# Key projection of a two-layer RWKV7/NSA kernel: one 512-column matmul per piece of high weight, halves summed by VectorE

## The chip, the cores and the metric

The kernel runs on one core of a Trainium2 chip. A core has a matmul engine (TensorE, PE in the profile; its weight loads are listed apart as PEld), three engines that compute on tiles (VectorE, DVE; ScalarE, ACT; GpSimd, POOL) and SyncE (SP), which here only issues transfers. The engines run side by side, each through its own instructions in order, and wait for one another through semaphores. Matmul results go to PSUM: eight banks, each of 512 float32 columns on 128 partitions. Everything else on the chip lies in SBUF.

The metric is the device time of one execution in microseconds. The time before is the median of three runs.

## The reference

256 tokens of width 2048 go through an RWKV7 layer, then an NSA attention layer that shares one set of keys and values, then a norm. The change lies in the RWKV7 layer, in the projection that makes the keys:

```
xx = token_shift(u) - u
mixed = u[None] + xx[None] * mu[:, None, None, :]
rkvz = jnp.einsum('nbtd,nde->nbte', mixed[:4], w_rkvz)
r, k, v, z = rkvz[0], rkvz[1], rkvz[2], rkvz[3]
...
kk = heads(k * k_k).astype(jnp.float32)
kk = kk / jnp.maximum(jnp.sqrt(jnp.sum(kk * kk, axis=-1, keepdims=True)), 1e-12)
k = k * (1.0 + (a - 1.0) * k_a)
...
o = wkv7_scan(rh, heads(decay), kh, vh, -kk, kk * ah.astype(jnp.float32))
```

Everything is float32. k has 2048 columns, that is 16 blocks of 128, two heads of 64 in each.

## The kernel before

**Products.** TensorE multiplies float32 in a rounded form (fp32r). To keep precision, each operand is split in two: a rounded, "high" part and the "low" rest. A product is the sum of three: high weight by high input, high weight by low input, low weight by high input. A weight piece arrives by DMA in a tile wraw; ScalarE writes its rounded copy whi (line 211) and VectorE the rest, wlo (line 190). Five pairs of whi and wlo exist, so the splitting runs some three pieces ahead of TensorE. For the inputs, function split_into makes the same two parts, and puts them side by side in one tile mx of 2 x 256 columns; the dictionary joint keeps that tile under the name of the projection and the 128-row piece k.

**Order of the work.** First all of v; then z block 0 (512 columns), the sixteen key blocks, z blocks 1 to 3, and then the scan, into which the projection of r is dealt. The list ZK holds that middle part. For one key block, cols_step runs four times, once for each 4 pieces of 128 rows; for each piece it issues three matmuls of 256 columns (tokens) into a 128 x 256 result with the weights stationary. cols_step also has a second form: given an output of 512 columns, it multiplies whi by the whole joint tile (512 columns: high and low input side by side), and wlo by the high input into the first 256 columns. The z blocks of the second layer use that form already, and VectorE adds the two halves behind it (line 1733).

**Key stage.** When a key block is done, stage_k takes it up: it copies it out of PSUM (ksb), squares it (sqk), sums squares by head on TensorE (rn, line 699), takes the power -0.5 (line 707 VectorE, 708 GpSimd), spreads it (rnx, line 714 ScalarE and 717 TensorE), and makes the tile sp of scaled keys, decays and inverse decays (lines 720 to 737, on VectorE, ScalarE and GpSimd), of which TensorE makes products ab (line 744). Stage j begins when block j is done and stage j - 2 has made its ab. The stages of several blocks overlap with the next blocks' matmuls.

**Triangular inverse.** When stages 0 to 7 are through, stage_t(0) reads their products back from DRAM (invA) and inverts triangular 32 x 32 matrices with small VectorE instructions (inverse_ops, line 774); its result goes out to DRAM (tnd, yvd) and comes back for the scan (Yb, line 883, used by TensorE at line 998). stage_t(1) does the same for blocks 8 to 15.

**What sets the order of instructions.** The generator code runs under a small planner, Sched, that interleaves stages, mixing of inputs (lines 426, 427, 433) and matmuls by planned costs. On top of it the framework's scheduler simulates the engines in time and lays out the final order of each engine. So a changed instruction can move others on all engines.

**PSUM.** In this part, acc tiles turn through banks 2, 0 and 1. Two key blocks share one bank: block j in the first 256 columns if j is even, in the last 256 if it is odd. A z block takes two banks. When a z block is done, ScalarE and VectorE evacuate it (close_z, line 647).

## Time and profile before

| | us |
|---|---|
| Median of three runs | 1145.06 |
| Lowest, highest | 1141.73, 1147.56 |
| Profiled execution, its own time | 1145.28 |
| Its span in the profile | 1143.5 |
| First key block's first matmul starts | 144.4 |
| Last key block's last matmul of the first kind (line 595) starts | 276.6 |
| The scan's first matmul of line 998 starts | 365.3 |

The page of a profile gives the busy time of each engine and its share of the span. A matmul row of a timeline gives its start and its length; the lengths of neighbouring matmuls overlap, since they are pipelined. "PEclk" is the clock that TensorE was granted, as a share of full speed. In square brackets stands the time that an engine sat idle before an instruction, and what ended it. A row with "x16: 361/366/375" gives the count, and the least, median and longest duration in ns.

### The profile page before, as it was taken

The numbers are of one execution on the slowest core, as the hardware profiler recorded it, in microseconds if no ns is written. First come the engines' busy times: TensorE is split into PE (matmuls) and PEld (weight loads), VectorE is DVE, ScalarE is ACT, GpSimd is POOL, SyncE is SP. The second block draws the span as 40 slices with busy tenths as digits, with TensorE's granted clock in tenths as the row PEclk, the third lists the DMA queues.
The fourth block names the chain that finished last, engine by engine and source line by source line (L and its number), as shares of the span: only waits on it lengthen the run. The fifth ranks groups of instructions, "written<-read, shape, count | busy, mean of one in ns | idle before, by whom it ended". The sixth has DMA issues, their size and how long they took to land.

```text
span 1143.5 us, 24949 instructions
## 1 busy us (share of the span) xinstructions
PE 1113.6 (97%) x9136; PEld 962.9 (84%) x9136; DVE 864.4 (76%) x1807; ACT 715.3 (63%) x1680; POOL 346.9 (30%) x443
## 2 busy tenths in 40 slices
PE   8999999999999999999999999999999999999997
PEld 7788899988688988888778888787889988888787
DVE  7999976779978986556666877675576888988564
ACT  5667777767655465556556766664666666666553
POOL 1400045554434365444110010100334344452212
PEclk9999999999999999999999999999999999999999
DMA  6568978885899978665457758585756453748462
GB/s 227 169 189 233 250 205 245 227 219 173 265 282 276 240 196 236 170 172 137 139 183 224 234 166 284 164 291 167 187 152 162 117 149 105 198 108 283 166 194 102
DMA packets 238522, 225.37 MB, mean 197 GB/s; under 512 B 57541, under 2 KB 184821, under 8 KB 238400
## 3 DMA queue, kind: packets, MB, share of 16 engines
q1 hardware_dynamic: 233120, 217.17, 65.0%
q0 software_dynamic: 5280, 6.61, 2.1%
q8 instruction: 72, 1.18, 0.5%
q14 instruction: 50, 0.41, 0.1%
HBM read 200.48 MB, written 23.10 MB: 196 GB/s over the span
## 4 chain that ended last, share of the span: by engine, by line
PE 62%; DVE 5%; DMA 2%; issue 2%; ACT 1%; POOL 1%; POOLq 0%; ACTq 0%; DVEq 0%
PE bank L576 9%; PE bank L577 9%; PE bank L579 9%; PE bank L601 5%; PE bank L1285 3%; PE bank L602 3%; PE bank L241 2%; DMA Yb<-yvd 2%; PE bank L1286 2%; PE bank L1287 2%; DVE wlo L190 2%; PE pair L1304 2%; PE pair L1306 1%; PE pair L1305 1%; PE pair L241 1%
## 5 line engine op out<-in xcount | busy, mean ns | idle before, releaser
L190 DVE TENSOR_TENSOR wlo<-wraw,whi 128x512 fp32r<-128x512 f32 (+2 forms) x616 | 448.9, 744 | 150.4 <-ACT whi L211 147.8
L211 ACT ACTIVATE whi<-wraw 128x512 fp32r<-128x512 f32 (+2 forms) x664 | 402.7, 620 | 232.9 <-PE bank L579 91.7
L577 PE MATMUL bank<-wlo,mx 128*128 128x512 f32 (+3 forms) x576 | 217.8, 380 | 3.5 <-DVE wlo L190 2.6
L579 PE MATMUL bank<-whi,mx 128*128 128x512 f32 (+3 forms) x576 | 215.0, 376 | 0.0
L576 PE MATMUL bank<-whi,mx 128*128 128x512 f32 (+3 forms) x576 | 186.5, 377 | 1.3 <-ACT whi L211 0.5
L577 PEld LDWEIGHTS bank<-wlo,mx 128*128 128x128 f32 x576 | 108.7, 189 | 22.8 <-DVE wlo L190 5.4
L576 PEld LDWEIGHTS bank<-whi,mx 128*128 128x128 f32 x576 | 107.9, 189 | 19.1 <-ACT mx L1869 1.2
L579 PEld LDWEIGHTS bank<-whi,mx 128*128 128x128 f32 x576 | 108.7, 189 | 16.2 <-POOL mx L1870 0.4
L190 POOL TENSOR_TENSOR wlo<-wraw,whi 128x512 fp32r<-128x512 f32 (+2 forms) x48 | 63.1, 1316 | 110.6 <-ACT whi L211 88.7
L601 PE MATMUL bank<-mx,whi 128*128 128x512 f32 x240 | 86.8, 398 | 0.0
L595 PE MATMUL bank<-mx,whi 128*128 128x256 f32 (+1 forms) x288 | 85.0, 295 | 0.3 <-ACT mx L426 0.3
L596 PE MATMUL bank<-mx,whi 128*128 128x256 f32 (+1 forms) x288 | 82.3, 286 | 0.0
L597 PE MATMUL bank<-mx,wlo 128*128 128x256 f32 (+1 forms) x288 | 81.7, 286 | 0.0
L1285 PE MATMUL bank<-mx,whi 128*128 128x256 f32 x256 | 81.6, 319 | 0.0
L577 PE MATMUL bank<-wlo,kvh 128*128 128x512 f32 x192 | 76.9, 401 | 0.0
L579 PE MATMUL bank<-whi,kvl 128*128 128x512 f32 x192 | 76.1, 396 | 0.0
L1286 PE MATMUL bank<-mx,whi 128*128 128x256 f32 x256 | 72.9, 285 | 0.0
L1287 PE MATMUL bank<-mx,wlo 128*128 128x256 f32 x256 | 72.8, 284 | 0.0
L602 PE MATMUL bank<-mx,wlo 128*128 128x256 f32 x256 | 70.6, 285 | 0.2 <-DVE wlo L190 0.2
L576 PE MATMUL bank<-whi,kvh 128*128 128x512 f32 x192 | 67.4, 396 | 0.0
L426 ACT ACTIVATE mx<-mtmp 128x256 fp32r<-128x256 f32 x96 | 38.7, 413 | 31.1 <-DVE mtmp L433 30.8
L595 PEld LDWEIGHTS bank<-mx,whi 128*128 128x128 f32 (+1 forms) x288 | 54.0, 187 | 2.2 <-ACT mx L426 0.7
(344 smaller groups left out, 2393.8 us busy)
## 6 DMA issues: line engine op xcount, KB each, us to landing
wraw<-in_a_w_rkvz_dram SPq DMA_DIRECT2D x128, 512.0 KB, 5.4
wraw<-in_kv_w_dram SPq DMA_DIRECT2D x48, 512.0 KB, 4.4
wraw<-in_b_w_in_dram SPq DMA_DIRECT2D x40, 512.0 KB, 4.2
wraw<-in_a_w_o_dram SPq DMA_DIRECT2D x32, 512.0 KB, 4.6
wraw<-in_b_w_o_dram SPq DMA_DIRECT2D x32, 512.0 KB, 3.9
spd<-sp SPq DMA_DIRECT2D x16, 642.0 KB, 5.1
wraw<-in_b_w_in_dram SPq DMA_DIRECT2D x24, 384.0 KB, 3.4
spl<-spd SPq DMA_DIRECT2D x14, 642.0 KB, 7.2
```

Of the source, the lines that this page charges most:

```text
L190: eng.tensor_tensor(lv, src, hv.bitcast(F32), op=OP.subtract)
L211: self.nc.scalar.activation(hv, src, AF.Copy)
L576: PE.matmul(o, mh[:, ts], wh[:, 0, :], start=k == ends[0], stop=False)
L577: PE.matmul(o, mh[:, ts], wl[:, 0, :], start=False, stop=False)
L579: PE.matmul(o, ml[:, ts], wh[:, 0, :], start=False, stop=k == ends[1])
L595: PE.matmul(o, wh[:, s, :], mh, start=k == 0 and first, stop=False, **kw)
L596: PE.matmul(o, wh[:, s, :], ml, start=False, stop=False, **kw)
L601: PE.matmul(o, wh[:, s, :], joint[nm, k], start=k == 0, stop=False, **kw)
L602: PE.matmul(o[:, :T], wl[:, s, :], mh, start=False, stop=False, **kw)
L1285: PE.matmul(o, wh[:, s, :], mh, start=k == 0, stop=False)
L1286: PE.matmul(o, wh[:, s, :], ml, start=False, stop=False)
L1287: PE.matmul(o, wl[:, s, :], mh, start=False, stop=k == NK - 1)
```

## The change

The key blocks use the second form of cols_step. Each key block takes a whole bank: whi times the joint tile fills 512 columns, wlo times the high input adds to the first 256. VectorE's reduce adds the two halves into ksb in SBUF, and ScalarE squares ksb, where before ScalarE copied and squared the block from PSUM. Sixteen banks are turned through now in the key part, not eight, over the same three banks.

```diff
         pk = kps.pop(j)
         ksb = tmp("ksb")
         sqk = tmp("t1")
-        S.activation(ksb, pk, AF.Copy)
-        S.activation(sqk, pk, AF.Square, scale=KK[:, j:j + 1])
+        V.tensor_reduce(ksb, pk.rearrange("p (a t) -> p t a", a=2), axis=AX.X, op=OP.add)
+        S.activation(sqk, ksb, AF.Square, scale=KK[:, j:j + 1])
         rn = accp("rn")
...
-    kacc = []
-
     def phase_k(j):
         if j % 2 == 0:
             load_pair(j // 2)
-            kacc[:] = [accp("acc")]
-        o = kacc[0][:, (j % 2) * 256:(j % 2) * 256 + 256]
+        o = accp("acc")
         for q in range(4):
             yield from cols_step(o, "k", q)
```

The form of cols_step that the key blocks take now, and which was there before for the z blocks of the second layer:

```
end = k == NK - 1
if not end:
    PE.matmul(o, wh[:, s, :], joint[nm, k], start=k == 0, stop=False, **kw)
PE.matmul(o[:, :T], wl[:, s, :], mh, start=False, stop=False, **kw)
if end:
    PE.matmul(o, wh[:, s, :], joint[nm, k], start=False, stop=True, **kw)
```

Three lines fewer stand in the file from phase_k on, so line 774 of before is line 771 of after, and so forth.

The order of TensorE at the end of the first key block, before (bank_1777 is the block's bank, mx_1675 and mx_1693 the last two input pieces):

```order
L595 MATMUL bank_1777<-mx_1675,whi 128x256
L596 MATMUL bank_1777<-mx_1675,whi 128x256
L597 MATMUL bank_1777<-mx_1675,wlo 128x256
L595 MATMUL bank_1777<-mx_1693,whi 128x256
L596 MATMUL bank_1777<-mx_1693,whi 128x256
L597 MATMUL bank_1777<-mx_1693,wlo 128x256
L595 MATMUL bank_1777<-mx_1393,whi 128x256
```

And now, at the same place:

```order
L601 MATMUL bank_1777<-mx_1675,whi 128x512
L602 MATMUL bank_1777<-mx_1675,wlo 128x256
L602 MATMUL bank_1777<-mx_1693,wlo 128x256
L604 MATMUL bank_1777<-mx_1693,whi 128x512
L689 MATMUL bank_2050<-hw,w2s 128x256
L690 MATMUL bank_2050<-ha,w2s 128x256
L601 MATMUL bank_1830<-mx_1393,whi 128x512
```

Two matmuls stand where three stood, the last piece closes with the wide one, and the next block goes to another bank (1830) where before it went on in 1777.

The order of VectorE around the first key block's evacuation, before (the two zth rows evacuate z block 0; f, sst and cum belong to the key stage):

```order
L647 TENSOR_TENSOR zth<-bank_1545,zth 128x512
L190 TENSOR_TENSOR wlo<-wraw,whi 128x512 x4
L726 TENSOR_TENSOR f<-ksb,f 128x256
L707 TENSOR_SCALAR sst<-bank_1862 128x4
L711 SCALAR_TENSOR_TENSOR cum<-cst,thw 128x256
```

And now:

```order
L647 TENSOR_TENSOR zth<-bank_1545,zth 128x512
L190 TENSOR_TENSOR wlo<-wraw,whi 128x512 x3
L695 TENSOR_REDUCE ksb<-bank_1777 128x256
L190 TENSOR_TENSOR wlo<-wraw,whi 128x512
L726 TENSOR_TENSOR f<-ksb,f 128x256
L711 SCALAR_TENSOR_TENSOR cum<-cst,thw 128x256
```

The reduce of block 0 stands among the low weights, and the stage's small instructions change places behind it.

The order of VectorE at the end of z block 1, the first z block behind the keys, before (inv names are the triangular inverse, mx and mtmp the mixing of r, zth the evacuation of the z block):

```order
L774 TENSOR_TENSOR invX<-invT,invM 128x512
L190 TENSOR_TENSOR wlo<-wraw,whi 128x512
L433 SCALAR_TENSOR_TENSOR mtmp<-xx,prm,xn 128x256
L647 TENSOR_TENSOR zth<-bank_3811,zth 128x512
L647 TENSOR_TENSOR zth<-bank_3812,zth 128x512
L427 TENSOR_TENSOR mx_4323<-mtmp,mx_4323 128x256
L427 TENSOR_TENSOR mx_4362<-mtmp,mx_4362 128x256
L774 TENSOR_REDUCE invT<-invX 128x8x8
L427 TENSOR_TENSOR mx_4413<-mtmp,mx_4413 128x256
```

And now:

```order
L427 TENSOR_TENSOR mx_4165<-mtmp,mx_4165 128x256
L190 TENSOR_TENSOR wlo<-wraw,whi 128x512
L647 TENSOR_TENSOR zth<-bank_3563,zth 128x512
L771 TENSOR_TENSOR invX<-invA,invM_2757 128x512
L647 TENSOR_TENSOR zth<-bank_3564,zth 128x512
L771 TENSOR_REDUCE invM<-invX 128x8x8
L190 TENSOR_TENSOR wlo<-wraw,whi 128x512
L771 TENSOR_TENSOR invX<-invA,invM_2757 128x512
```

The mixing of r is through at that place, where before three pieces were left; the inverse has come less far: it reads invA here (the first of the last level's two products) where before it read invT (the second).

## The prediction

> **What bounds the kernel now.** First the page: its first two lines and the chain that ended last, to see which engine sets the end.
> ```profile
> span 1143.5 us, 24949 instructions
> PE 1113.6 (97%) x9136; PEld 962.9 (84%) x9136; DVE 864.4 (76%) x1807; ACT 715.3 (63%) x1680; POOL 346.9 (30%) x443
> PE 62%; DVE 5%; DMA 2%; issue 2%; ACT 1%; POOL 1%; POOLq 0%; ACTq 0%; DVEq 0%
> ```
> TensorE (PE) is busy for 1113.6 of 1143.5 us, so time is mostly saved by giving it less to do. That is an average, and the change touches only the sixteen key blocks and what stands behind them. So next the table by stretches, cut where the key blocks begin, where the triangular inverse's first VectorE instruction runs, where the z block behind the keys ends, where VectorE (DVE) gets air again, and where the last z block ends.
> ```profile
> core 0: us, PE busy (x) PEld busy (x) DVE busy (x) ACT busy (x) POOL busy (x), PEclk, DMA share, GB/s
> 144.20:235.60 91.40, 90.91 (x789) 86.11 (x788) 62.47 (x102) 68.49 (x163) 46.88 (x57) 1.00 0.83 227
> 235.60:311.10 75.50, 69.79 (x501) 59.40 (x500) 74.77 (x168) 53.23 (x127) 35.22 (x42) 1.00 0.72 211
> 311.10:320.00 8.90, 8.64 (x31) 6.62 (x31) 8.85 (x15) 4.31 (x8) 5.67 (x11) 0.81 1.08 305
> 320.00:353.70 33.70, 33.70 (x150) 27.91 (x149) 25.66 (x61) 19.70 (x34) 7.03 (x11) 1.00 0.93 268
> ```
> Two regimes. Up to 235.6 us TensorE runs without a gap (90.91 of 91.40) and VectorE has 28.93 us free: the bound is TensorE. From 235.6 to 311.1 VectorE is full (74.77 of 75.50), and TensorE stands for 5.71 us: the bound is VectorE. From 320 us TensorE is the bound again. The ends of the second stretch, and what it costs, in the timeline:
> ```profile
> 235.64 0.19 DVE L774 COPY invT<-invA 128x16 f32<-128x16 f32 x1 [3.33 <-DMA invA<-abd]
> 311.13 1.27 DVE L647 TENSOR_TENSOR zth<-bank,zth 128x512 f32<-128x512 f32 x2
> 309.66 0.50 PE L577 MATMUL bank<-wlo,mx 128*128 128x512 f32 x1 [0.76 <-DVE wlo L190]
> 311.86 0.63 PE L576 MATMUL bank<-whi,mx 128*128 128x512 f32 x1 [0.26 <-DVE zth L647]
> 312.29 0.63 PE L577 MATMUL bank<-wlo,mx 128*128 128x512 f32 x1
> ```
> TensorE waits for a low weight (wlo) and for the evacuation zth, and then its matmuls start 0.43 us apart (311.86, 312.29): the granted clock of 311.1 to 320 is 0.81. So lateness is paid twice there. Last the waits of TensorE from 235 to 320 us, longest first:
> ```profile
> PE bank L744 <- POOL sp L736: 2.7, 2, 2.1
> PE bank L577 <- DVE wlo L190: 1.5, 4, 0.8
> PE bank L717 <- ACT rnx L714: 1.3, 1, 1.3
> PE bank L576 <- DVE zth L647: 0.3, 1, 0.3
> ```
> Only 1.8 us (1.5 + 0.3) name VectorE itself. The other 4.0 are the key stage's own chain (key block, norm, rnx, nk, sp, L744), which passes VectorE's full queue three times; the change puts its reduce at the head of that chain.
>
> **What TensorE saves.** A step is one 128-row piece of one block: three matmuls of 256 columns now, one of 512 and one of 256 afterwards. Both forms stand in this trace, the new one in the z blocks of the second layer (L601, L602). The rows' first number is the start, and matmuls overlap, so the price is the distance of the starts.
> ```profile
> 276.49 0.28 PE L597 MATMUL bank<-mx,wlo 128*128 128x256 f32 x1
> 276.61 0.28 PE L595 MATMUL bank<-mx,whi 128*128 128x256 f32 x1
> 276.73 0.28 PE L596 MATMUL bank<-mx,whi 128*128 128x256 f32 x1
> 276.85 0.28 PE L597 MATMUL bank<-mx,wlo 128*128 128x256 f32 x1
> ...
> 1041.09 0.40 PE L601 MATMUL bank<-mx,whi 128*128 128x512 f32 x1
> 1041.32 0.28 PE L602 MATMUL bank<-mx,wlo 128*128 128x256 f32 x1
> 1041.44 0.40 PE L601 MATMUL bank<-mx,whi 128*128 128x512 f32 x1
> 1041.68 0.28 PE L602 MATMUL bank<-mx,wlo 128*128 128x256 f32 x1
> 1041.79 0.39 PE L601 MATMUL bank<-mx,whi 128*128 128x512 f32 x1
> ```
> Old step: 276.85 - 276.49 = 0.36 us. New step: (1041.79 - 1041.09) / 2 = 0.35 us. The columns streamed are the same 768; what goes is one start. So 0.01 us for each of 16 x 16 = 256 steps: **2.6 us**. The starts are printed to 0.01 us, so the difference may be 0.005 to 0.015: 1.3 to 3.8 us. At most 11 of the 16 blocks (1.8 us) lie before 235.6 us, where TensorE is the bound and the saving counts at once.
>
> [...]
>
> **What ScalarE loses.** The copy of the block out of PSUM goes, and the square reads the SBUF copy.
> ```profile
> L695 ACT ACTIVATE ksb<-bank x16: 361/366/375, 150.8 to 279.5; 128x256 f32<-128x256 f32 x16
> L696 ACT ACTIVATE t<-bank,prm x16: 462/467/478, 151.0 to 279.8; 128x256 f32<-128x256 f32 x16
> L732 ACT ACTIVATE sp<-f,prm x16: 492/510/527, 152.3 to 288.1; 128x256 f32<-128x256 f32 x16
> ```
> 16 x 0.366 = 5.9 us less on an engine that is busy for 68.49 of 91.40 and 53.23 of 75.50 us: worth nothing by itself. The square may grow a little: L732, of the same size with a scale column and both sides in SBUF, takes 0.510 where the square takes 0.467, 0.7 us for sixteen, hidden too.
>
> **What VectorE gains.** Sixteen reduces of 512 to 256 columns out of PSUM. The same instruction evacuates the z blocks of the second layer.
> ```profile
> L1733 DVE TENSOR_REDUCE zT<-bank x16: 673/681/692, 833.0 to 1044.1; 128x256 f32<-128x512 f32 x16
> ...
> 1036.24 0.68 DVE L1733 TENSOR_REDUCE zT<-bank 128x256 f32<-128x512 f32 x1
> 1036.84 0.18 DVE L1793 RECIPROCAL rc<-sm 128x6 f32<-128x6 f32 x1
> ```
> One lasts 0.681 us and the next instruction starts after 0.60 us, so 0.60 us of VectorE's time each, 9.6 us in all. In the new order eleven reduces stand ahead of the inverse's first instruction: 11 x 0.60 = 6.6 us, hidden by the 28.93 us free there (if that cover were gone, the weights' low halves would be 6.6 us late). Each reduce stands in VectorE's queue behind the low weights of the next block (the four of block 1 ahead of block 0's reduce), so while it waits for its own block's last matmul it holds back nothing that TensorE needs in the block after. The other **five, 3.0 us**, fall into the full stretch.
>
> But the order that the scheduler lays out has other work moved in that stretch, too. Between the inverse's first instruction and the first zth I count in the two orders: inverse 66 then 59, low weights 37 then 35, mixing of r 26 then 29, small work of the key stage 39 then 35, reduces 0 then 5. The seven inverse pieces that now stand behind zth are those of 128x512:
> ```profile
> 309.53 0.68 DVE L774 TENSOR_TENSOR invX<-invT,invM 128x512 f32<-128x512 f32 x1
> 310.13 0.68 DVE L190 TENSOR_TENSOR wlo<-wraw,whi 128x512 fp32r<-128x512 f32 x1
> 310.73 0.47 DVE L433 SCALAR_TENSOR_TENSOR mtmp<-xx,prm,xn 128x256 f32<-128x256 f32 x1
> ```
> These rows give 0.60 us (309.53 to 310.13, 310.13 to 310.73) for an inverse piece and for a low weight, and 0.40 (to zth at 311.13) for a mixing piece and, as an upper bound, for a small one. The reduces, the inverse and the mixing give +3.0 - 7 x 0.60 + 3 x 0.40 = **0.0 us**. The two low weights and four small pieces (2 x 0.60 + 4 x 0.40 = 2.8 us) merely moved ahead of the inverse's start, so they come off no total. Bounds: all five reduces unpaid, +3.0; two more low weights' progress won, -2.8. I take 0: VectorE neither loses nor wins there, and what remains is TensorE's earlier arrival.
>
> What is late next is the inverse. Its last piece stands behind low weight 187 instead of 182. TensorE uses six matmuls for one low weight, 6 x 33.70 / 150 = 1.35 us by the table's last row, so 5 x 1.35 = 6.7 us later. Its readers:
> ```profile
> 323.96 1.22 DVE L774 TENSOR_REDUCE invT<-invX 128x64 f32<-128x1024 f32 x1
> L883 SPq DMA_DIRECT2D Yb<-yvd x8: 303/441/642, 338.0 to 343.1; - x8
> L998 PE MATMUL pair<-Yb,a x256: 192/219/240, 365.3 to 537.0; 64*64 64x32 f32 x128
> ```
> The load of Yb goes out 14 us after the last piece (323.96 to 338.0), and TensorE uses it at 365.3. A delay of 6.7 us is inside that margin. SyncE's queue, where weight loads stand behind the Yb load, would be held by it only once the delay passes those 14 us less the stores between. I cost it at nothing.
>
> **Sum.** 2.6 saved on TensorE, of which I take 2.0 as kept (the 1.8 us before 235.6 us and a part of the rest), nothing on ScalarE, nothing net on VectorE: **-2.0 us**. The profiled execution took 1145.28 us (1143.5 of span and 1.8 around it), 0.2 above the median of three, 1145.06. Forecast: 1145.28 - 2.0 = 1143.3 us.
>
> **Rivals.**
> *VectorE eats the gain.* If the full stretch keeps all the inverse's pieces in front of what TensorE waits for in effect, the five reduces push zth 3.0 us out and only the 1.8 us won before remain: 1145.28 + 3.0 - 1.8 = 1146.5 us. For it: the 74.77 of 75.50. Against it: the seven pieces moved behind zth.
>
> *The full stretch relaxes.* If the moved inverse pieces take VectorE off the bound there, some 0.6 of the 5.71 us of standing go (my guess between a third, the 1.8 us that name VectorE, and all), and the lost clock behind zth too, (1 - 0.81) x 8.90 = 1.7 us: 1145.28 - 2.6 - 0.6 x 5.71 - 1.7 = 1137.6 us. For it: those pieces are exactly the work that nobody needs yet. Against it: the mixing of r, as little needed, stays in front.
>
> *Slower: VectorE stands at the reduces.* VectorE's queue is in order. In the full stretch low weights, the inverse and the key stage's own products stand behind a reduce, which must wait for its block's last matmul. The plan was made with planned times; if TensorE reaches that matmul 1.4 us (about one low weight's worth) after VectorE reaches the reduce, five such waits cost 7 us, with 3.0 for the reduces and one more stretch of lost clock, 1.7, less 2.6 saved: 1145.28 + 9.1 = 1154.4 us. It decides from the point where VectorE catches up with TensorE; in the full stretch it has been behind, so this needs the plan to err the other way.
>
> *A 512-column matmul as cheap as one of 256.* If streaming overlapped so far that a wide matmul costs one start, each step would take 0.24 us: 256 x 0.12 = 31 us less, 1114.6 us. The rows speak against it: 1041.09 to 1041.32 is 0.23 for the wide one. [...]
>
> **How the numbers follow.** Forecast 0.50; VectorE eats the gain 0.28; the stretch relaxes 0.12; slower 0.09; the cheap wide matmul 0.01. About 0.5%, 5.7 us, is what a measurement of this kernel can tell from no change. The forecast and the first rival lie inside it; of the second rival three quarters lie beyond it, with the last rival 0.10 for faster; the slower one, whole, and a little of the first give 0.10; 0.80 stay within. The forecast's own range is the bounds of its terms: the saving (-3.8 to -1.3) and -2.8 to +3.0 for the full stretch, 1138.7 to 1147.0. The first rival, with nothing won before 235.6 us and the square's 0.7 added, reaches 1149; so 1139.0 to 1149.0, leaving out the slower rival and the far part of the two fast ones.
>
> **What would show it.** Right, if the new L601 to L601 distance in the key blocks is 0.35 us, the eleven key blocks before the inverse's start take 1 to 2 us less, TensorE's idle time from there to zth is again near 5.7 us, and the reduces last 0.68 us with no wait ahead of them on VectorE in the full stretch. Wrong, if waits of TensorE for L190 or zth grow by more than 3 us, if a reduce shows idle time released by TensorE in the full stretch, or if the scan's first L998 waits for Yb.

## The result, and the profile after

The changed kernel takes 1156.17 us (median of five; 1150.82 to 1158.62) where the kernel before takes 1145.06. The ratio is 1.0098, with a 95% interval of 1.0073 to 1.0124: 11 us slower. The forecast was 1143.3, the range 1139.0 to 1149.0; the time lies outside it. The profiled execution took 1152.86 us, 1151.1 of them span.

First the page's lines, as before:

```profile
span 1151.1 us, 24448 instructions
PE 1116.0 (97%) x8880; PEld 951.8 (83%) x8880; DVE 871.3 (76%) x1823; ACT 709.3 (62%) x1664; POOL 347.1 (30%) x443
PE 58%; DVE 6%; issue 4%; DMA 3%; ACT 2%; POOL 2%; SPq 0%; POOLq 0%; ACTq 0%; DVEq 0%
```

There are fewer matmuls (8880 for 9136), yet TensorE is busy for longer. The table by stretches, with the prediction's cuts and one more at the end, says where:

```profile
core 0: us, PE busy (x) PEld busy (x) DVE busy (x) ACT busy (x) POOL busy (x), PEclk, DMA share, GB/s
144.20:235.60 91.40, 89.57 (x606) 75.57 (x604) 68.22 (x114) 62.42 (x145) 45.01 (x56) 1.00 0.80 220
235.60:311.10 75.50, 69.06 (x402) 55.28 (x401) 70.03 (x165) 52.40 (x126) 34.79 (x37) 0.95 0.70 196
311.10:320.00 8.90, 8.90 (x39) 6.69 (x39) 5.26 (x10) 2.50 (x5) 6.92 (x15) 0.68 0.90 273
320.00:353.70 33.70, 33.70 (x150) 27.89 (x150) 26.74 (x45) 19.92 (x33) 8.11 (x14) 1.00 0.98 272
353.70:380.00 26.30, 21.10 (x170) 19.51 (x171) 20.59 (x58) 11.13 (x21) 10.12 (x17) 0.87 0.98 274
```

The last row of the kernel before, by the same view:

```profile
353.70:380.00 26.30, 25.72 (x375) 24.30 (x374) 24.12 (x57) 13.34 (x27) 14.24 (x25) 1.00 1.07 276
```

Two things are new. TensorE no longer runs without a gap up to 235.6 us (1.83 us free where there were 0.49). And the granted clock (third number from the end) falls to 0.95, 0.68 and 0.87 where it was 1.00, 0.81 and 1.00. TensorE's waits from 235 to 320 us, and from 320 to 380:

```profile
PE bank L744 <- POOL sp L736: 3.5, 3, 2.3
PE bank L717 <- ACT rnx L714: 2.1, 2, 1.4
PE bank L699 <- ACT t L696: 1.1, 1, 1.1
PE bank L577 <- DVE wlo L190: 0.3, 1, 0.3
...
PE bank L1282 <- DVE vt L647: 4.6, 1, 4.6
PE pair L1021 <- ACT bkt L1024: 0.6, 1, 0.6
```

From 320 to 380 us the kernel before has the last of these alone:

```profile
PE pair L1024 <- ACT bkt L1027: 0.6, 1, 0.6
```

The waits for low weights and zth, which the prediction watched, shrank from 1.8 to 0.3 us. The key stage's own waits grew from 4.0 to 6.7, and one of 4.6 us is new, at the first matmul of r's projection. It is the largest single loss, and the prediction had not thought of it:

```profile
361.73 0.68 DVE L647 TENSOR_TENSOR vt<-bank,vt 128x512 f32<-128x512 f32 x1
...
362.47 0.58 PE L1282 MATMUL bank<-mx,whi 128*128 128x256 f32 x1 [4.62 <-DVE vt L647]
362.85 0.42 PE L1283 MATMUL bank<-mx,whi 128*128 128x256 f32 x1
363.06 0.42 PE L1284 MATMUL bank<-mx,wlo 128*128 128x256 f32 x1
```

vt is the evacuation of the last z block (z3). TensorE wants z3's bank for r, and VectorE empties it late. Behind the wait the matmuls start 0.21 us apart instead of 0.12. The windows around the three stretches of half clock, TensorE alone (length, busy, count, granted clock):

```profile
251.99:255.40 3.41, 1.76 (x20) 1.00 0.66 189
255.40:258.82 3.42, 2.95 (x12) 0.50 0.91 213
258.82:262.23 3.41, 3.41 (x12) 0.50 0.78 202
262.23:265.64 3.41, 3.41 (x20) 1.00 0.47 154
306.60:310.02 3.42, 1.21 (x5) 0.99 0.45 156
310.02:313.43 3.41, 3.20 (x20) 0.50 0.50 176
313.43:316.84 3.41, 3.41 (x9) 0.50 0.93 179
357.81:361.22 3.41, 0.04 (x1) 0.99 1.16 291
361.22:364.63 3.41, 2.16 (x10) 0.50 1.16 290
364.63:368.05 3.42, 3.42 (x18) 0.51 1.09 365
```

Cut in steps of 3.41 us from the right point, each of the three windows in which TensorE stands long (busy for 1.76, 1.21 and 0.04 us) is followed by two whole windows at half clock. At the granted 0.50 each of those costs up to half of 3.41, an estimated 1.7 us; six of them make 10.2 us, where the kernel before has one between 140 and 400 us. (Part of one passes while TensorE stands anyway, as at 361.22, so the 10.2 and the waits may not be added up.)

How the lateness builds up can be read from the starts of a few instructions in the two traces (us):

| | before | changed | later by |
|---|---|---|---|
| Key block 11, first matmul | 232.31 | 230.47 | -1.8 |
| Key block 15, first matmul | 269.16 | 271.15 | 2.0 |
| VectorE's first zth of z block 1 | 311.13 | 312.98 | 1.9 |
| r's first matmul, less its wait for vt | 353.71 | 357.85 | 4.1 |
| r's first matmul | 353.71 | 362.47 | 8.8 |
| The first matmul that reads Yb | 365.31 | 376.61 | 11.3 |

Up to block 11 the changed kernel is ahead by what the prediction counted on; all of the loss comes behind that.

### The profile page after: what moved, and what is told of

Read it like the earlier page. It is cut to its first block, busy times and chain, and to the rows that moved or that the text cites. A ratio compares the mean times of both kernels' runs of the same rounds, so it can differ in the third digit from the quotient of the medians.

```text
span 1151.1 us, 24448 instructions
## 1 busy us (share of the span) xinstructions
PE 1116.0 (97%) x8880; PEld 951.8 (83%) x8880; DVE 871.3 (76%) x1823; ACT 709.3 (62%) x1664; POOL 347.1 (30%) x443
## 4 chain that ended last, share of the span: by engine, by line
PE 58%; DVE 6%; issue 4%; DMA 3%; ACT 2%; POOL 2%; SPq 0%; POOLq 0%; ACTq 0%; DVEq 0%
PE bank L577 8%; PE bank L579 8%; PE bank L576 8%; PE bank L601 5%; PE bank L1282 3%; DVE wlo L190 3%; PE bank L602 3%; PE bank L241 2%; PE bank L1283 2%; PE bank L1284 2%; DMA Yb<-yvd 2%; PE pair L1301 2%; PE pair L1303 1%; PE pair L1302 1%; PE pair L241 1%
## 5 line engine op out<-in xcount | busy, mean ns | idle before, releaser
L577 PE MATMUL bank<-wlo,mx 128*128 128x512 f32 (+3 forms) x576 | 218.6, 381 | 3.1 <-DVE wlo L190 2.0
L601 PE MATMUL bank<-mx,whi 128*128 128x512 f32 x480 | 179.1, 408 | 0.0
L602 PE MATMUL bank<-mx,wlo 128*128 128x256 f32 x512 | 141.8, 287 | 0.2 <-DVE wlo L190 0.2
L601 PEld LDWEIGHTS bank<-mx,whi 128*128 128x128 f32 x480 | 91.5, 191 | 18.0
L602 PEld LDWEIGHTS bank<-mx,wlo 128*128 128x128 f32 x512 | 97.9, 191 | 4.3 <-DVE wlo L190 0.7
L1284 PE MATMUL bank<-mx,wlo 128*128 128x256 f32 x256 | 73.1, 285 | 0.0
L1282 PEld LDWEIGHTS bank<-mx,whi 128*128 128x128 f32 x256 | 49.5, 193 | 8.8 <-DVE vt L647 5.0
L1283 PEld LDWEIGHTS bank<-mx,whi 128*128 128x128 f32 x256 | 50.1, 196 | 0.0
```

What stands on the lines that cost most here:

```text
L577: PE.matmul(o, mh[:, ts], wl[:, 0, :], start=False, stop=False)
L601: PE.matmul(o, wh[:, s, :], joint[nm, k], start=k == 0, stop=False, **kw)
L602: PE.matmul(o[:, :T], wl[:, s, :], mh, start=False, stop=False, **kw)
L1282: PE.matmul(o, wh[:, s, :], mh, start=k == 0, stop=False)
L1283: PE.matmul(o, wh[:, s, :], ml, start=False, stop=False)
L1284: PE.matmul(o, wl[:, s, :], mh, start=False, stop=k == NK - 1)
```

## The experiments

All ratios are against runs of the kernel before on the same chip. Since one profiled execution differs from another by some microseconds outside the changed part, the last column gives a local measure from the traces: from VectorE's first zth (the evacuation of z block 0) to the first matmul of the scan that reads Yb. The kernel before has 218.6 us there (146.7 to 365.3), the changed one 229.9, so the loss arises in this part.

| label | what differs | ratio [95% interval] | local, us |
|---|---|---|---|
| (the change) | | 1.0098 [1.0073, 1.0124] | 229.9 |
| e1_rot | change, z blocks in the banks of before | 1.0061 [1.0040, 1.0082] | 224.8 |
| e2_badrot | before, z blocks in the banks of the change | 1.0021 [1.0000, 1.0042] | 219.7 |
| e3_dvecopy | before, VectorE copies the blocks | 1.0053 [1.0030, 1.0076] | 220.3 |
| e4_wide_act | e1, ScalarE evacuates one half | 1.0011 [0.9992, 1.0031] | 218.2 |
| e6_load | e4 and an unread reduce on VectorE | 1.0042 [1.0026, 1.0057] | 221.6 |
| e5_split | e1, ScalarE and VectorE share the sum | 1.0043 [1.0025, 1.0061] | 221.8 |
| e7_narrow_bank | before, a bank for each block | 0.9994 [0.9976, 1.0011] | 216.9 |
| e16_copy_bank | e7, VectorE copies the blocks | 1.0030 [1.0014, 1.0047] | 219.6 |
| e14_sum_early | e4, VectorE sums blocks 0 to 10 | 1.0028 [1.0009, 1.0047] | 219.1 |
| e15_sum_late | e4, VectorE sums blocks 11 to 15 | 1.0060 [1.0037, 1.0083] | 222.3 |
| e8_klag3 | e1, three stages in flight | 1.0058 [1.0033, 1.0082] | 223.6 |
| e9_warm | e4 and idle matmuls | 1.0106 [1.0089, 1.0124] | 225.8 |
| e13_warm_sum | e1 and idle matmuls | 1.0118 [1.0096, 1.0140] | 226.9 |
| e18_sq_dve | e1, VectorE squares too | 1.0138 [1.0107, 1.0169] | 225.8 |
| e19_sq_pool | e1, GpSimd squares | 1.0089 [1.0056, 1.0123] | 224.0 |
| e11_pool | e1, 8 low weights on GpSimd | 1.0055 [1.0038, 1.0071] | 220.6 |
| e12_pool_narrow | e7, 8 low weights on GpSimd | 1.0116 [1.0097, 1.0136] | 227.6 |
| e20_rmix_pool | before, r's low parts on GpSimd | 1.0103 [1.0076, 1.0129] | 226.2 |

**The turn of the banks.** Sixteen turns over three banks end one bank from where eight turns end. So z3 lies in banks 0 and 1, and r's projection begins in just those; before, it lay in 1 and 2. e1 sets the turn back behind the keys, e2 shifts it in the kernel before (with 2 for 1):

```diff
     for nm, i in ZK:
+        if (nm, i) == ("z", 1):
+            turn["acc"] += 1
```

> The changed kernel, but the turn of the three banks is advanced by one ahead of z block 1, so that the z blocks and the scan get the same banks as in the kernel before. Theory A (bank turn): z block 3 lay in banks 0 and 1 in the changed kernel, which the scan's projection of r needs at once, so TensorE stood 4.6 us for vt and then ran some 4 us at half clock. Then the wait for vt is gone, the first r matmul comes 0.2 us behind the last z matmul, and the time is 4 to 7 us under the changed kernel's 1156.2: 1149 to 1152. Rival B (all of the loss comes from the key stage, and the scan takes up the wait anyway, since its Yb loads have less to wait for then): under 1.5 us less, 1155 to 1156.

> The kernel before, with the turn of the banks advanced by two ahead of z block 1, so that z block 3 lies in banks 0 and 1 as in the changed kernel. Nothing else is edited. Theory A: TensorE waits 4 to 5 us for vt ahead of the scan, and the time is 4 to 7 us over the kernel before: 1149 to 1152. Rival B: within 1.5 us of 1145.

e1 is 0.37% faster than the change, 4.2 us (5.1 by the local measure), as theory A forecast, and its wait for vt is gone (one of 2.0 us for a low weight stands behind it instead). In e2 the wait appears:

```profile
PE bank L1287 <- DVE vt L647: 3.0, 1, 3.0
```

It costs only 2.4 us there (0 to 4.8 by the interval), between the two forecasts: VectorE reaches vt at 355.10 us, not 361.73, and no half clock follows. So the bank turn makes the wait, and by these two traces the lateness of VectorE decides its price.

**Who evacuates.** In place of ScalarE's copy and square from PSUM, e3 (two blocks a bank) and e16 (a bank for each) have VectorE's copy with narrow matmuls; e4 has ScalarE with wide ones (first half only); e7 is the narrow kernel with a bank for each block and e1's turn.

```diff
 e3, e16
-        S.activation(ksb, pk, AF.Copy)
-        S.activation(sqk, pk, AF.Square, scale=KK[:, j:j + 1])
+        V.tensor_copy(ksb, pk)
+        S.activation(sqk, ksb, AF.Square, scale=KK[:, j:j + 1])
 e4
-        V.tensor_reduce(ksb, pk.rearrange("p (a t) -> p t a", a=2), axis=AX.X, op=OP.add)
-        S.activation(sqk, ksb, AF.Square, scale=KK[:, j:j + 1])
+        S.activation(ksb, pk[:, :256], AF.Copy)
+        S.activation(sqk, pk[:, :256], AF.Square, scale=KK[:, j:j + 1])
 e7, e16
-        o = kacc[0][:, (j % 2) * 256:(j % 2) * 256 + 256]
+        o = accp("acc")[:, :256]
```

> The kernel before (narrow matmuls, two blocks a bank), with one part of the change: VectorE copies the key block out of PSUM, 256 columns, and ScalarE squares the copy. Theory C (the evacuation at the head of the key stage's chain now stands in VectorE's queue): waits of TensorE in the key blocks for t, rnx and sp (lines 699, 717, 744) grow from 4.5 to 6 us or more, some with half clock behind; time 2 to 4 us over before, 1147 to 1149. Rival D (only the length of the reduce counts, and a copy of 256 columns at about 0.34 us each is hidden): within 1 us of 1145.

> The wide matmul and one bank a block, with the bank turn of e1_rot, but ScalarE evacuates as before, and the first 256 columns alone; the product of high weight and low input in the second half is left out of ksb. This is the change without VectorE's part. If the wide matmul saves its 0.01 us a step and the banks are right, TensorE's 2.6 us come through: 1142 to 1143.5. If instead the order that the scheduler makes of a shorter key block is itself worse (waits of TensorE in the key blocks over 6 us), 1146 or more.

> The kernel before with its three narrow matmuls and ScalarE's copy and square, but with one bank for each key block instead of one for two, and the banks turned back behind the keys: the wide matmul is all that the wide kernel with ScalarE's copy (+1.3 us) has beyond it. If the wide matmul's 2.6 us do not come through since TensorE only waits more for the key stage: 0 to +2 us over the kernel before, 1144.4 to 1146.4. If they do come through, and the bank of its own for each block costs what was won: +3 to +4.5 us, 1147.4 to 1149, with more waits of TensorE from 144 to 311 us than before (6.3 us).

> Narrow matmuls, a bank for each block, the banks turned back, and VectorE's copy of the block (0.42 us) in place of ScalarE's, the square from the copy. Beside the same kernel with ScalarE's copy (-0.6 us) it gives the price of the evacuation by VectorE without wide matmuls a second time, and beside the changed kernel with its banks turned back (+7.0 us) what the wide matmul is worth where VectorE evacuates. If the evacuation costs 5 to 6 us whatever the matmuls' form, and the wide matmul again wins nothing: +4.5 to +6 us over the kernel before. If the wide matmul's 2.6 us come through where VectorE evacuates: +7.5 to +9.5.

VectorE in place of ScalarE costs 0.50% with wide matmuls (e1 less e4), 0.53% (e3) and 0.36% (e16 less e7) with narrow ones: 4 to 6 us, three times. The wide matmul itself wins nothing in either pair: e4 less e7 is +0.17%, e1 less e16 +0.31% (in the second pair the reduce is also longer than the copy, 0.68 to 0.42 us). And a bank of its own for each block costs nothing (e7). Of the forecasts, e3's were both too low (+6.1 us came); e4 lies between its two, and e7 (-0.7) and e16 (+3.4) lie a little below the nearer of theirs.

Why the wide matmul's gain does not come through, e4 shows beside the kernel before (the rows of 200 to 235 and 235 to 260 us, e4's first, then the kernel before's):

```profile
200.00:235.00 35.00, 33.51 (x237) 28.25 (x234) 22.92 (x40) 24.84 (x64) 18.01 (x24) 1.00 0.79 216
235.00:260.00 25.00, 21.89 (x135) 18.62 (x136) 20.33 (x59) 17.86 (x47) 11.48 (x15) 0.88 0.89 226
```
```profile
200.00:235.00 35.00, 35.00 (x307) 32.96 (x307) 23.80 (x39) 27.60 (x68) 19.43 (x25) 1.00 0.84 228
235.00:260.00 25.00, 22.71 (x201) 20.93 (x200) 23.96 (x66) 17.18 (x43) 14.49 (x17) 1.00 0.71 201
```

The gain is there at first. Block 11 begins 84.8 to 86.1 us after the first key matmul in twelve of the thirteen kernels with wide matmuls (87.5 in e13, which has idle matmuls added), and 87.6 to 87.9 us in the seven with narrow ones. It is lost behind that. In e4 TensorE begins block 13 102.7 us after the first key matmul, the kernel before 107.2: e4 is 4.5 us ahead. Then it waits for sp (2.0 us at 252.2) and rnx (1.0 at 255.0), runs at half clock from 254 to 261 us, and needs 14.3 us for that block instead of 9.0. The work in between is the key stage's, which lags: from a block's square to ScalarE's copy of its products ab it took 17.5 to 27 us in e4 for the blocks 0 to 12, and 12.7 to 18.3 before. The wide form's order puts the stage's steps later; why the scheduler does so was not tried.

**How much is VectorE's load, how much the chain.** e6 adds the reduce to e4, into a tile that nobody reads. e5 shortens VectorE's part. e8 lets three stages overlap (KLAG = 3).

```diff
 e6
+        V.tensor_reduce(kdm, pk.rearrange("p (a t) -> p t a", a=2), axis=AX.X, op=OP.add)
 e5
-        V.tensor_reduce(ksb, pk.rearrange("p (a t) -> p t a", a=2), axis=AX.X, op=OP.add)
+        S.activation(ksb, pk[:, 256:], AF.Copy)
+        V.tensor_tensor(ksb, pk[:, :256], ksb, op=OP.add)
```

> The kernel with the wide matmul in which ScalarE copies and squares the first half from PSUM (1145.2 us beside a kernel before of 1144.4), and with one thing more: VectorE makes its reduce of 512 to 256 columns out of PSUM for each block as in the changed kernel, but into a spare tile that nobody reads. So VectorE's load is that of the changed kernel, and the key stage's chain does not pass through the reduce. Like the kernel that it is made from, it leaves out the product of high weight by low input in the keys' result. Theory load (the 9.6 us of VectorE time cost what they cost because VectorE is full from 235 to 311 us, whatever they feed): as slow as the changed kernel with its banks turned back, +5 to +6 us over the kernel before, 1149.5 to 1150.5. Theory chain (the cost is that the reduce stands at the head of each block's chain of norm, rnx, nk, sp and ab, and waits there in VectorE's queue): +1 to +2 us, 1145 to 1146.5, with the square starting as early as in the kernel that it is made from. A value in the middle, 1147 to 1148.5, says that both take a share.

> The changed kernel with its banks turned back, in which the halves are summed by two engines: ScalarE copies the second half out of PSUM, VectorE adds the first half to it (256 columns instead of 512 read). VectorE's instruction should last about 0.40 us instead of 0.68, which leaves it 16 x some 0.25 = 4 us lighter, while the chain gets a ScalarE copy (0.37 us) ahead of the VectorE instruction. Theory load: 40 per cent of the 5.7 us of the evacuation comes back, +3.5 us over the kernel before, 1147.5 to 1148.5. Theory chain: nothing comes back, since the chain still passes VectorE and has got one step longer, +6 to +7 us, 1150 to 1152.

> The changed kernel with its banks turned back, in which the stage of key block j may begin when the stage of block j - 3 has made its products, instead of j - 2. If the longer chain costs because each stage must wait for the one two blocks back: 2 to 4 us of the 5.9 come back, 1146 to 1148.5, with fewer and shorter waits for rnx and sp (L717, L744). If it costs because VectorE's time is short in the full stretch, this changes nothing, 1149 to 1151.5.

e6 costs 3.0 to 6.5 us over the kernel before, by its interval: the +5 to +6 of the load theory lie in it, the +1 to +2 of the chain theory do not. By the points, load alone takes 0.31 of the 0.50%; whether it takes all of it the intervals cannot tell, and VectorE also stood 5.5 us in e6 ahead of the unread reduce, behind the square, which e1 does not have. e5, with 6.7 us of VectorE's time for 10.9, gets 0.18% back, less than the intervals can tell from nothing; at +4.9 us it lies between its two forecasts and decides nothing. In e8 the 2 to 4 us that were to come back did not: the gate of two stages is not the bound.

**Early or late.** e14 and e15 divide the reduces at block 11, as the prediction did (e15 with `j >= 11` in the first line).

```diff
+        if j < 11:
+            V.tensor_reduce(ksb, pk.rearrange("p (a t) -> p t a", a=2), axis=AX.X, op=OP.add)
+            S.activation(sqk, ksb, AF.Square, scale=KK[:, j:j + 1])
+        else:
+            S.activation(ksb, pk[:, :256], AF.Copy)
+            S.activation(sqk, pk[:, :256], AF.Square, scale=KK[:, j:j + 1])
```

> The kernel with wide matmuls and the banks turned back, in which VectorE's reduce evacuates the blocks 0 to 10, and ScalarE copies and squares the first half of the blocks 11 to 15 (for these it leaves out the product of high weight by low input). The two ends are known: ScalarE for all sixteen +1.3 us over the kernel before, VectorE for all sixteen +7.0 us. If the first eleven reduces are hidden by VectorE's 28.93 free us before the inverse, as the prediction has it: +1 to +2.5 us. If a reduce costs the same wherever it stands (since it is its place at the head of the chain that costs): 1.3 + 11/16 of 5.7 = +5.2 us, +4 to +6.5.

> The counterpart: ScalarE copies and squares the first half of the blocks 0 to 10, VectorE's reduce evacuates the blocks 11 to 15. If the price of the reduces lies in the stretch where VectorE is full: +5.5 to +7.5 us over the kernel before. If a reduce costs the same wherever it stands: 1.3 + 5/16 of 5.7 = +3.1 us, +2 to +4.2.

The five late ones alone cost 0.49% over e4, as much as all sixteen, and +6.9 us over the kernel before, as the first forecast for e15 says; the eleven early ones 0.17%, with intervals that overlap e4's (+3.2 us over the kernel before lies between the two forecasts). Only some of the late price arises in the stretch itself. By the traces, counted from the first key matmul, the last zth of z block 1 comes 1.7 us later in e15 than in e4 (170.1 for 168.4), r's first matmul 1.0 us later (209.8 for 208.8), and the first matmul that reads Yb 4.2 us later (224.6 for 220.4). So most of it arises behind r's first matmul, where VectorE must also do the second triangular inverse. The last long instruction of the first inverse and the start of the second in the changed kernel:

```profile
334.73 1.21 DVE L771 TENSOR_REDUCE invT<-invX 128x64 f32<-128x1024 f32 x1
...
352.33 0.18 DVE L771 COPY invT<-invA 128x16 f32<-128x16 f32 x1 [1.25 <-DMA invA<-abd]
```

and the second's start in the kernel before:

```profile
340.23 0.18 DVE L774 COPY invT<-invA 128x16 f32<-128x16 f32 x1
```

The first inverse's last long instruction comes 10.8 us later (334.73 for 323.96), and 5.3 of these are there when the inverse starts (240.93 for 235.64); e4, without reduces, starts it at 240.71 too. The second inverse starts 12.1 us later, right where vt, zt and r's first low weights are due. In the other traces what counts is how far it starts ahead of r's first matmul. Where that is 8.6 us or more (the kernel before, e2, e4, e7, e9, e11, e12, e13, e14, e16, e19, e20), TensorE waits 0 to 0.2 us for a low weight at the start of r; at 6.5 us (e5, e3) it waits 1.0 and 1.3, at 3.7 to 4.4 us (e8, e6, e15, e1) 2.0 to 2.5. Only e18, at 1.2 us, does not fit: it waits 0.4 for a low weight and 1.1 for a high one. In e15 twelve pieces of the inverse stand on VectorE from 362.44 us on, behind zt and ahead of the low weight that TensorE waits for:

```profile
365.66 0.68 DVE L190 TENSOR_TENSOR wlo<-wraw,whi 128x512 fp32r<-128x512 f32 x1
366.39 0.39 PE L1290 MATMUL bank<-mx,wlo 128*128 128x256 f32 x1 [2.49 <-DVE wlo L190]
```

**Is it the half clock?** e9 and e13 give TensorE idle work near its waits.

```diff
+        for _ in range(2 if j >= 9 else 0):
+            PE.matmul(ab[:, 256:512], at[:, :128], at, start=True, stop=True)
```

> The kernel with the wide matmul in which ScalarE copies and squares the first half (+1.3 us over the kernel before; leaves out the product of high weight by low input in the keys), with idle work added on TensorE: for the blocks 9 to 15, two float32 matmuls of 128x256 ahead of L744, from the tile of scaled keys into columns of the ab bank that nobody reads. I estimate 0.44 us for each by L689, which has 256 columns of float32 and starts 0.44 us ahead of L690; 14 x 0.44 = 6.2 us more work for TensorE. Theory clock (the wide matmul's gain is given back as half clock: that kernel's trace has one stretch, 254 to 261 us, at half clock, which costs 3.42 us, behind waits for sp and rnx): the added work runs in the waits, TensorE no longer falls to half clock between 235 and 300 us, and the time is 1 to 3 us less than without it, -1.5 to +0.5 us over the kernel before. Theory waits (the waits themselves are the price, and the clock is a side effect): the added 6.2 us come in place of the waits at best, 0 to +4 us on top of the 1.3, so +1.3 to +5 us.

> The changed kernel with its banks turned back (VectorE sums the halves, +7.0 us over the kernel before), with the same idle work on TensorE for the blocks 9 to 15: two float32 matmuls of 128x256 ahead of L744. Its trace without them lost 6.8 us to half clock between 250 and 374 us, of which 5.1 lie in the key part. Theory clock: some 3 us of these come back, +3 to +5 us over the kernel before. Theory waits: +7 to +11 us.

Half clock from 140 to 400 us fell (lost time 3.42 to 1.71 us in e9, 6.83 to 5.12 in e13), and the time rose by 0.95 and 0.57% all the same. Over the kernel before that is +12.1 and +13.5 us, more than either theory forecast. The added matmuls keep TensorE busy for 8.2 us in e9 and 7.2 in e13. In e9 they did not run inside the waits: from 235 to 320 us these add up to 7.0 us, where e4 has 7.3, and 1.8 of the 7.0 are new ones, for sp, at the idle matmuls themselves. In e13 they fell to 3.7 from 7.0 in e1, and the time rose too. So these waits are not free room. What half clock costs by itself the two runs do not show, since the added work has a price of its own.

**Does ScalarE's queue carry it?** In the changed kernel ScalarE stands at its square for VectorE's reduce, and rnx, on which TensorE waits 1.36 us right after, is queued behind:

```profile
255.00 0.51 ACT L696 ACTIVATE t<-ksb,prm 128x256 f32<-128x256 f32 x1 [3.74 <-DVE ksb L695]
255.41 0.40 ACT L714 ACTIVATE rnx<-rnt 128x256 f32<-128x256 f32 x1
...
255.87 0.69 PE L717 MATMUL bank<-cst,rnx 128*128 128x128 f32 x2 [1.36 <-ACT rnx L714]
```

e18 and e19 take the square from ScalarE (its scale goes into L699's matrix); e18 has VectorE make it, e19 GpSimd:

```diff
-        S.activation(sqk, ksb, AF.Square, scale=KK[:, j:j + 1])
+        V.tensor_tensor(sqk, ksb, ksb, op=OP.mult)
```

> The changed kernel with its banks turned back (+7.0 us over the kernel before), in which VectorE also makes the square, right behind its reduce, as a plain product of ksb with itself; the scale that the square had goes into the small matrix of L699, once for each block at the program's start (16 small VectorE instructions). So ScalarE has nothing left that waits for the reduce: its square stood 3.05 and 3.74 us for it at 245.6 and 255.0 us in the changed kernel's trace, with rnx and the next rounded weights queued behind. VectorE gets 16 x about 0.34 = 5.4 us more to do (by L731, 128x256 from SBUF, 0.34 to the next start). Theory queue (the price of the late reduces is that ScalarE, which waits for them in order, holds up rnx and the weights): 2 to 4 us come back, +3 to +5 us over the kernel before, and no wait of ScalarE for ksb. Theory load (the price is VectorE's time in the full stretch): some 2 to 4 us more, +9 to +11 us.

> The same with the square on GpSimd, some 1.0 us each by L736 and L737 of the kernel before: neither ScalarE nor VectorE has more to do than without the change's square, but GpSimd stands for the reduce in order, with the power L708 and the products L736 and L737 queued behind, and the chain gets some 0.5 us longer. Theory queue: what ScalarE wins GpSimd loses in the same way, +5 to +8 us over the kernel before. Theory load: ScalarE's part is no bound and VectorE's load is unchanged, so +6 to +8 us, as without the edit; the two theories are told apart by the kernel with VectorE's square, this one only tells whether moving the wait to another queue helps.

With ScalarE free of that wait, e18 is 0.77% slower than e1. The queue theory's forecast fell. The load theory has the sign, but forecast 2 to 4 us and 8.8 came; the square took 0.62 us on the mean (median 0.42, longest 0.97), 9.9 us in all where 5.4 were planned, so a small gain from ScalarE's queue could be hidden in it. e19, with the square on GpSimd, is 0.28% slower than e1, which the intervals cannot tell from nothing.

**Taking load away.** e11 and e12 give GpSimd eight low weights, e20 r's low parts:

```diff
 e11, e12
+    W.on_pool.update(range(128, 152, 3))
 e20
-        V.tensor_tensor(l, src, h.bitcast(F32), op=OP.subtract)
+        (G if nm == "r" else V).tensor_tensor(l, src, h.bitcast(F32), op=OP.subtract)
```

> The changed kernel with its banks turned back (+7.0 us), in which every third low weight of the key blocks 10 to 15, eight in all, is made by GpSimd instead of VectorE. That takes 8 x 0.60 = 4.8 us off VectorE, half of what the sixteen reduces put on it, and adds 8 x 1.3 = 10.5 us to GpSimd. Theory load (most of the evacuation's price is VectorE's time in the full stretch from 235 to 311 us): 2 to 4 us come back, +3 to +5 us over the kernel before. Theory chain (the price is the wait of the chain): nothing comes back, or the low weights on GpSimd hold the products of sp (L736, L737) back, +7 to +10 us.

> The kernel with narrow matmuls, ScalarE's copy and square, a bank for each block and the banks turned back (-0.6 us against the kernel before), with the same eight low weights on GpSimd. It tells whether the relief of VectorE is worth something without the reduces. If VectorE is the bound of the full stretch already in the kernel before: 2 to 4 us less, -2.5 to -4.5 us. If GpSimd holds the key stage back, or the low weights come late to TensorE: 0 to +4 us.

> The kernel before, unchanged in the keys, with the low parts of r's mixed inputs (L427, sixteen of 128x256, which nobody needs before the scan) made by GpSimd instead of VectorE: 16 x about 0.40 = 6.4 us less on VectorE, most of it between 235 and 311 us, and 16 x about 1.0 us more on GpSimd (by L1870, the same form there). Theory load, in the other direction: between 0.5 and 0.7 us of time for each us of VectorE's work, as the kernels with ScalarE's evacuation, VectorE's evacuation and VectorE's evacuation and square show (+1.3, +7.0, +15.8 us for 0, 10.9 and 20.8 us of it), so 3 to 4.5 us faster than the kernel before, and faster than both kernels. Rival: GpSimd's queue, in order, holds the key stage's power and products (L708, L736, L737) back by about 1 us at a time, as the low weights on GpSimd seem to have done: 0 to +4 us.

All three missed. e20 should have beaten both kernels and lost 12 us. VectorE's groups from 235 to 311 us, e20's first, then those of the kernel before (busy, mean ns):

```profile
L190 DVE TENSOR_TENSOR wlo<-wraw,whi 128x512 fp32r<-128x512 f32 x33 | 28.4, 871 | 0.0
L433 DVE SCALAR_TENSOR_TENSOR mtmp<-xx,prm,xn 128x256 f32<-128x256 f32 x13 | 9.6, 739 | 0.0
```
```profile
L190 DVE TENSOR_TENSOR wlo<-wraw,whi 128x512 fp32r<-128x512 f32 x37 | 27.4, 746 | 0.0
L433 DVE SCALAR_TENSOR_TENSOR mtmp<-xx,prm,xn 128x256 f32<-128x256 f32 x13 | 7.6, 586 | 0.0
```

The same instructions became longer: 33 x 0.125 + 13 x 0.153 = 6.1 us, as much as the 6.4 that were taken away. So e20 relieved VectorE of next to nothing and says nothing on the load theory. Its own 11.8 us are explained in part only: TensorE's waits from 235 to 320 us grew from 5.8 to 8.2 us (for sp, the rival's sign, from 2.7 to 3.6), and 2.6 us for high weights came behind. e12's low weights were as long (872 ns); why e11, with 754, did not suffer like e12 stays open.

## Why the prediction was wrong, step by step

By the ratios the loss of 11.2 us divides into 4.2 for the turn of the banks (change less e1), 5.7 for the evacuation by VectorE (e1 less e4) and 1.3 for the rest (e4). Each ratio is uncertain by 2 to 3 us, so the first two shares are by some 3 to 4, and the 1.3 cannot be told from nothing.

- **The turn of the banks** is in no step: the sixteen turns are named in the change, but no step asks where z3 comes to lie behind them. This is the first failure, an omission: 4.2 us.
- **The later inverse, "I cost it at nothing"**, failed. It was to end 6.7 us later and ended 10.8 us later, 5.3 of them there at its start, and the margin was counted for the load of Yb alone. The second inverse, which follows, slid 12.1 us into the beginning of r. That it delays r's low weights there, e15 shows; that it also delays vt (361.73 us for 355.83 before, 1.8 us more than r itself is late), and so raises the price of the bank wait, is read from the traces and was not tested alone.
- **"VectorE neither loses nor wins there"**, the net 0.0 for the five late reduces, failed with it: e15 puts 5.6 us on them. The prediction set seven inverse pieces against the reduces; these had only been put off, behind z block 1, and were still to be paid there.
- **The eleven early reduces are hidden**: borne out within the uncertainty (0.17%).
- **2.6 us on TensorE, 2.0 kept**: the size was right (the next rows give 165.04 - 164.69 = 0.35 us a step), and so was "counts at once": the 1.8 us were won when block 11 began. Their keeping was wrong. By block 15 the changed kernel is 2.0 us behind, and no pair of kernels shows a gain. In the full stretch TensorE runs ahead of its key stage and waits for that.

```profile
164.69 0.39 PE L601 MATMUL bank<-mx,whi 128*128 128x512 f32 x1
164.92 0.28 PE L602 MATMUL bank<-mx,wlo 128*128 128x256 f32 x1
165.04 0.39 PE L601 MATMUL bank<-mx,whi 128*128 128x512 f32 x1
```

- **Durations** held: the reduce 682 ns, the square 500 where up to 510 was allowed.

```profile
L695 DVE TENSOR_REDUCE ksb<-bank 128x256 f32<-128x512 f32 x16 | 10.9, 682 | 1.0 <-PE bank L604 1.0
L696 ACT ACTIVATE t<-ksb,prm 128x256 f32<-128x256 f32 x16 | 8.0, 500 | 7.3 <-DVE ksb L695 7.0
```

- **The rivals.** "VectorE eats the gain" had the right engine and no loss behind zth, 1146.5. "VectorE stands at the reduces" had nearly the right time, 1154.4, for a wrong reason: its five reduces in the full stretch waited 0.0 us. That nearness is luck. None of the three signs that were to show the prediction wrong appeared, and those that were to show it right did: 0.35 us a step, the eleven blocks 1.8 us shorter, reduces of 0.68 us that wait for nothing in the full stretch, and 6.4 us of idle time up to zth, near the 5.7. The loss came from places that none of them watched.

What stays open: how the 5.6 us of the late reduces divide between VectorE's time, the stage's chain and half clock; e6 and e18 speak for VectorE's time as the larger part, e5 decides nothing, and no run lowered VectorE's time cleanly. No kernel here beats the kernel before; e7 is even with it.

## What to carry to other kernels

When a change alters how many buffers a ring hands out, follow the ring to its next user: who gets the bank that the last evacuation holds? When work goes onto a full engine, pieces that slide behind a deadline are not won; follow each to its reader and to the next instance of the same job. And time saved on an engine is kept only as far as the work that it meets next is ready.

## What the runs showed of the hardware

In all twenty traces every change of the granted clock between full and half lies within 0.03 us of a grid of 3.413 us, whose phase differs from execution to execution. Of the windows at full clock with TensorE busy under 40%, 27 of 27 were followed by a slower one; at 40 to 65%, 38 of 74; at 65 to 75%, 7 of 82; above, 2 of 6337 (the end of each trace left out). In the changed kernel half clock followed a window with 1.76 us of work in 3.41 (251.99 to 255.40).

VectorE's low weights of 128x512 (two inputs from SBUF) often took longer while GpSimd's products (lines 736, 737) ran. Between 140 and 330 us 18 of 97 took over 1.0 us in the kernel before and 12 of 95 in the changed one, and each of these lies inside products for 0.48 of its length or more. Of those that lie inside products for 0.8 of their length or more, 10 of 16 took over 1.0 us before and 4 of 19 in the changed kernel; inside the small power (line 708) it is none of 5 and none of 8, and of the 56 and 54 that lie wholly outside both none took over 0.70. In e20, with r's low parts on GpSimd too, the low weights from 235 to 311 us took 871 ns on the mean, 746 in the kernel before. In the kernel before, GpSimd's product runs from 299.92 to about 301.92 us (its spans are rough); the mixing piece at 300.37 and the low weight at 301.25 took 0.95 and 1.22 us, where 0.47 (as at 310.73, shown in the prediction) and 0.67 are usual:

```profile
299.77 0.67 DVE L190 TENSOR_TENSOR wlo<-wraw,whi 128x512 fp32r<-128x512 f32 x1
300.37 0.95 DVE L433 SCALAR_TENSOR_TENSOR mtmp<-xx,prm,xn 128x256 f32<-128x256 f32 x1
301.25 1.22 DVE L190 TENSOR_TENSOR wlo<-wraw,whi 128x512 fp32r<-128x512 f32 x1
```
```profile
299.92 2.00 POOL L736 TENSOR_TENSOR sp<-an,pinv 64x256 f32<-64x256 f32 x2 [7.09 <-DVE an L731]
```

In these rows that is 2.0 and 1.8 times; the cause was not shown. The reduce, whose input is in PSUM, stayed at 0.67 to 0.69 us, also in the ten of the changed kernel's sixteen that lie inside GpSimd's products or power for 0.8 of their length or more.
